# Two hybrid transformer blocks in one kernel: the pool of the weights begins 64 bytes further in SBUF

## Chip, cores and metric

One Trainium2 chip, one core. The metric is the device time of one execution in microseconds (us). The kernel before takes 2362.53 us, the median of 3 runs (2360.72 to 2367.87). The compute engines are called by their names in the profile: PE (TensorE; PEld is its weight load, the LDWEIGHTS instruction that goes ahead of each matmul), DVE (VectorE), ACT (ScalarE), POOL (GpSimd); SP is the engine from whose queue the weights' transfers are issued.

## What is computed

256 tokens of width 1024 go through two layers of a first block and two of a second, all in float32. Cut to what matters here (the attention branches in between are left out):

```python
for l in range(2):                                   # first block
    h = rms(x, ln1[l]) * (1 + sc1) + sh1
    x = x + g1 * mixing(h @ w_in[l], ...) @ w_o[l]
    h = rms(x, ln2[l]) * (1 + sc2) + sh2
    x = x + g2 * ((silu(h @ w_gate[l]) * (h @ w_up[l])) @ w_down[l])
for l in range(2):                                   # second block, 256 tokens and 256 of a context
    h, hc = norm(x) * (1 + scale) + shift, norm(ctx) * (1 + scale_c) + shift_c
    parts, parts_c = split(h @ w_in[l]), split(hc @ w_in[l])
    y = g_a * (y_a @ w_a_out[l]) + g_b * (y_b @ w_b_out[l]) + g_c * (y_c @ w_c_out[l])
    x = x + gate * (y @ w_out[l])
```

Nearly all of the work is in the dense products with `w_in`, `w_o`, `w_gate`, `w_up`, `w_down`, and the second block's `w_in`, `w_*_out`, `w_out`.

## The kernel before

**Dense products.** Every factor of a dense product is held as two tiles of type fp32r, a rounded part (`hi`) and the rest (`lo`), and a product is the sum of three matmuls per 128 rows of the contraction: hi·hi, hi·lo, lo·hi (`mm3`, L559). All matmuls go through one recording helper, so that the profile shows L170 for each; they are told apart by their tiles. In a name such as `ps_mm<-h,whi`, the first tile behind the arrow is the one that streams through the array (the moving operand), the second the one that was loaded as weights (the stationary operand).

- `dense_t` (L570): 128 columns of the weights are stationary, the inputs move, 256 or 512 columns wide (`ps<-h,whi`). It is used for the first block's `w_o`, `w_gate`, `w_up`, `w_down`, for part of its `w_in`, and for most of the second block.
- `dense_n` (L576): 128 tokens of the inputs are stationary, 256 columns of the weights move (`ps<-whi,h`). It is used for those projections that are wanted token by token.

**Tiles and where they lie.** A block of weights is fetched by SP into one of two `raw` tiles (`fetch`, L356), and then split in two halves (`split_half`, L381): ACT rounds `raw` into `whi`, DVE (sometimes POOL) writes `raw - whi` into `wlo`. There are two of each, 8192 bytes per partition, all six in the pool `w` (L1854). The normed inputs of all dense products lie in `h2`, two tiles of 16384 bytes (L1866), in a pool that is stacked from the other end of SBUF, as are the tiles of the feed-forward part (`ahi`, `alo`, L1175), the gated branches (`part`) and the merged output (`fhi`, `yacc`). The pools opened behind `w` on its own side (conditioning, masks, `dft`, `u`, `pq`, the attention tiles of the left side) follow it in the stack.

All block sizes and steps of these tiles are multiples of 512 bytes, so that the byte at which a matmul's operand starts, modulo 512, is the same for every block of a tile. In the program these bytes are:

| tile | start modulo 512 | distance from the weights, around 512 |
|---|---|---|
| `whi`, `wlo`, `raw` | 160 | |
| `h` (a slice of `h2`), `part`, `fhi`, `yacc` | 480 | 192 |
| `ahi`, `alo`, first block's layer 0 | 288 | 128 |
| `ahi`, `alo`, first block's layer 1 | 384 | 224 |
| `dft`, `u`, `pq` (they meet each other only) | 64 | (0 from each other) |

**The order of the work.** While the program is built, a planner (`Clock`, L66, and `Pipe`, L222) keeps a modelled time for each engine and decides from it in which order instructions are written to the queues. It knows tiles by name and by offsets inside a tile; where a tile lies in SBUF does not enter.

The function that the diff touches, and its callers:

Of the kernel before, what the change touches and what calls it, by code (L numbers as in the profile page):

```python
# [7 lines left out]
F32 = mybir.dt.float32  # L8
# [295 lines left out]
class Program:  # L304
# [1544 lines left out]
    def run(self):  # L1849
# [2 lines left out]
        self.const = self.stack.enter_context(self.pool("const"))  # L1852
        self.x = self.const.tile([128, KC, L], F32, name="xT")
        self.wp = self.stack.enter_context(self.pool("w"))  # L1854
        self.gbufs = 4
        self.gw = None
        self.dram = self.stack.enter_context(tc.tile_pool(name="dram", bufs=1, space=bass.MemoryType.DRAM))
# [216 lines left out]
```

## Time and profile before

| | |
|---|---|
| median of 3 runs | 2362.53 us |
| the profiled execution, own time | 2364.57 us |
| its span, first to last instruction | 2362.8 us |
| mean granted TensorE clock | 0.969 of full speed |
| PE, PEld busy | 2247.8 us (95%), 1974.9 us (84%) |
| DVE, ACT, POOL busy | 1287.4 (54%), 1032.1 (44%), 371.7 us (16%) |

A matmul's duration in the profile (mean ns) runs from its start to the modelled end of its results, and the next one begins while it still runs. So the quantity to read is the pace: the time from the start of one matmul to the start of the next, in an unbroken stretch a window's length by its number of matmuls. A window counts every matmul that overlaps it, so that two or three at its ends are counted too many (280 ns of duration against a pace below 120 ns).

### The profile page before, as it was taken

The numbers are of one execution on the slowest core, as the hardware profiler recorded it, in microseconds if no ns is written. First come the engines' busy times: TensorE is split into PE (matmuls) and PEld (weight loads), VectorE is DVE, ScalarE is ACT, GpSimd is POOL, SyncE is SP. The second block draws the span as 40 slices with busy tenths as digits, with TensorE's granted clock in tenths as the row PEclk, the third lists the DMA queues.
The fourth block names the chain that finished last, engine by engine and source line by source line (L and its number), as shares of the span: only waits on it lengthen the run. The fifth ranks groups of instructions, "written<-read, shape, count | busy, mean of one in ns | idle before, by whom it ended". The sixth has DMA issues, their size and how long they took to land. (4 is left out here: it accounts for less than half of the span.)

```text
span 2362.8 us, 39015 instructions
## 1 busy us (share of the span) xinstructions
PE 2247.8 (95%) x15672; PEld 1974.9 (84%) x15672; DVE 1287.4 (54%) x2547; ACT 1032.1 (44%) x1994; POOL 371.7 (16%) x897
## 2 busy tenths in 40 slices
PE   7989999998899999997989999999999999989999
PEld 3756899876899988887878888888898897989999
DVE  3735556575556546666554424335364656655665
ACT  3543445445444444554543323223254445444543
POOL 3311001551000103122022000000020333220000
PEclk8978999998999999998999999999999999999999
DMA  9646985655686522122114434434343232337865
GB/s 331 230 159 220 288 252 181 212 188 196 197 243 187 173 89 72 56 82 72 61 65 139 128 91 113 119 94 114 96 131 90 81 99 74 106 114 201 211 172 170
DMA packets 395061, 348.52 MB, mean 148 GB/s; under 512 B 12768, under 2 KB 364384, under 8 KB 394368
## 3 DMA queue, kind: packets, MB, share of 16 engines
q1 hardware_dynamic: 386752, 321.29, 45.1%
q0 software_dynamic: 6688, 21.66, 2.9%
q10 hardware_dynamic: 1440, 3.08, 0.4%
q8 instruction: 123, 2.02, 0.4%
q14 instruction: 58, 0.48, 0.1%
HBM read 335.50 MB, written 10.49 MB: 146 GB/s over the span
## 5 line engine op out<-in xcount | busy, mean ns | idle before, releaser
L170 DVE TENSOR_TENSOR wlo<-raw,whi 128x1024 fp32r<-128x1024 f32 (+1 forms) x465 | 547.6, 1210 | 449.1 <-ACT whi L170 447.8
L170 ACT CAST whi<-raw 128x1024 fp32r<-128x1024 f32 (+3 forms) x476 | 471.5, 1031 | 216.1 <-PE ps_t L170 63.3
L170 PE MATMUL ps_mm<-whi,h 128*128 128x256 f32 x2752 | 533.9, 291 | 16.1 <-ACT whi L170 6.2
L170 PEld LDWEIGHTS ps_mm<-whi,h 128*128 128x128 f32 x2752 | 440.6, 194 | 48.7 <-issue 19.3
L170 PE MATMUL ps_mm<-wlo,h 128*128 128x256 f32 x1376 | 391.1, 284 | 7.5 <-DVE wlo L170 7.3
L170 PE MATMUL ps_mm<-h,whi 128*128 128x256 f32 (+2 forms) x1656 | 375.5, 321 | 1.9 <-DVE xT L170 1.8
L170 PEld LDWEIGHTS ps_mm<-h,whi 128*128 128x128 f32 (+1 forms) x1656 | 269.2, 187 | 46.9 <-issue 9.0
L170 PEld LDWEIGHTS ps_mm<-wlo,h 128*128 128x128 f32 x1376 | 266.8, 194 | 12.6 <-DVE wlo L170 8.4
L170 PE MATMUL ps_mm<-h,wlo 128*128 128x256 f32 (+2 forms) x828 | 263.0, 318 | 1.1 <-POOL wlo L170 1.1
L170 PE MATMUL ps_s<-h,whi 128*128 128x256 f32 (+1 forms) x1120 | 240.2, 310 | 0.0
L170 PE MATMUL ps_t<-h,whi 128*128 128x256 f32 (+1 forms) x1096 | 234.9, 310 | 2.1 <-ACT h L170 1.5
L170 PEld LDWEIGHTS ps_s<-h,whi 128*128 128x128 f32 x1120 | 181.3, 188 | 18.3 <-ACT th L170 5.6
L170 PEld LDWEIGHTS ps_t<-h,whi 128*128 128x128 f32 x1096 | 179.0, 190 | 19.8 <-ACT th L170 6.3
L170 PE MATMUL ps_s<-h,wlo 128*128 128x256 f32 (+1 forms) x560 | 173.4, 310 | 0.1
L170 PE MATMUL ps_t<-h,wlo 128*128 128x256 f32 (+1 forms) x548 | 169.5, 309 | 0.0
L170 PEld LDWEIGHTS ps_mm<-h,wlo 128*128 128x128 f32 (+1 forms) x828 | 155.1, 187 | 14.7 <-POOL wlo L170 1.3
L170 PE MATMUL ps_g<-gw,c 128*32 128x512 f32 (+1 forms) x640 | 100.8, 640 | 18.0 <-DMA gw<-in_w_mod_dram 8.7
L170 PEld LDWEIGHTS ps_s<-h,wlo 128*128 128x128 f32 x560 | 105.2, 188 | 7.0 <-DVE wlo L170 0.3
L170 PEld LDWEIGHTS ps_t<-h,wlo 128*128 128x128 f32 x548 | 104.2, 190 | 6.2 <-DVE wlo L170 0.2
L170 ACT ACTIVATE M<-ps_s,nmB,rsB 128x512 f32<-128x512 f32 (+1 forms) x96 | 67.0, 702 | 94.2 <-DVE nmB L170 94.2
L170 DVE SCALAR_TENSOR_TENSOR y<-th,y 128x512 f32<-128x512 f32 (+1 forms) x64 | 35.6, 556 | 81.2 <-ACT th L170 67.9
L170 POOL TENSOR_TENSOR sqa<-sqa,sq 128x256 f32<-128x256 f32 x30 | 22.1, 736 | 346.9 <-ACT sq L170 191.3
(406 smaller groups left out, 3726.8 us busy)
## 6 DMA issues: line engine op xcount, KB each, us to landing
raw<-in_w_in_dram SPq DMA_DIRECT2D x72, 1024.0 KB, 5.3
raw<-in_w_in_dram SPq DMA_DIRECT2D x100, 512.0 KB, 4.1
gw<-in_w_mod_dram SPq DMA_DIRECT2D x96, 512.0 KB, 5.3
gw<-in_w_ada_dram SPq DMA_DIRECT2D x64, 384.0 KB, 5.0
raw<-in_w_gate_dram SPq DMA_DIRECT2D x44, 512.0 KB, 4.1
raw<-in_w_up_dram SPq DMA_DIRECT2D x44, 512.0 KB, 5.6
raw<-in_w_down_dram SPq DMA_DIRECT2D x16, 1024.0 KB, 5.1
raw<-in_w_out_dram SPq DMA_DIRECT2D x12, 1024.0 KB, 5.2
```

Of the source, the lines that this page charges most:

```text
L170: return real(*a, **k)
```

## The change

One tile of 16 float32 per partition, 64 bytes, is allocated as the first of the pool `w`. Nothing reads or writes it. The six tiles of the weights, and everything that is stacked behind them on their side, lie 64 bytes further; the tiles on the other side stay. Weights then start at 224 modulo 512, and `h`, `part`, `fhi` and `yacc`, still at 480, are 256 bytes from them.

```diff
         self.x = self.const.tile([128, KC, L], F32, name="xT")
         self.wp = self.stack.enter_context(self.pool("w"))
+        self.wp.tile([128, 16], F32, name="apart")
         self.gbufs = 4
```

## Rows read from the trace of the kernel before

**Rows 1.** The page, parts 1 and 2: busy time, and PE in 40 slices.
```profile
PE 2247.8 (95%) x15672; PEld 1974.9 (84%) x15672; DVE 1287.4 (54%) x2547; ACT 1032.1 (44%) x1994; POOL 371.7 (16%) x897
...
PE   7989999998899999997989999999999999989999
...
PEclk8978999998999999998999999999999999999999
```

**Rows 2.** Groups of instructions by shape, PE: matmuls with weights; busy us, mean ns.
```profile
L170 PE MATMUL ps_mm<-whi,h 128*128 128x256 f32 x2752 | 533.9, 291 | 16.1 <-ACT whi L170 6.2 <-ACT h L170 5.5 <-DVE pq L170 2.1
L170 PE MATMUL ps_mm<-wlo,h 128*128 128x256 f32 x1376 | 391.1, 284 | 7.5 <-DVE wlo L170 7.3 <-POOL wlo L170 0.2
L170 PE MATMUL ps_mm<-h,whi 128*128 128x256 f32 x1112 | 203.9, 284 | 1.9 <-DVE xT L170 1.8
L170 PE MATMUL ps_mm<-h,whi 128*128 128x512 f32 x512 | 161.6, 397 | 0.0
...
L170 PE MATMUL ps_s<-h,wlo 128*128 128x256 f32 x408 | 113.8, 279 | 0.1
...
L170 PE MATMUL ps_s<-alo,whi 128*128 128x256 f32 x132 | 37.1, 281 | 0.0
...
L170 PE MATMUL ps_t<-alo,whi 128*128 128x256 f32 x110 | 30.9, 281 | 0.0
...
L170 PE MATMUL ps_mm<-part,whi 128*128 128x256 f32 x144 | 25.6, 278 | 0.0
...
L170 PE MATMUL ps_mm<-part,wlo 128*128 128x512 f32 x56 | 22.0, 392 | 0.0
...
L170 PE MATMUL ps_s<-part,wlo 128*128 128x256 f32 x56 | 15.6, 279 | 0.0
```

**Rows 3.** The chain of waits, pieces in order of time: start us, us, what.
```profile
2203.03 2.83 PE ps_mm L170 x24
...
2318.55 2.72 PE ps_t L170 x24
```

**Rows 4.** Unbroken stretches of PE: window, its length, PE busy (count), granted clock, DMA.
```profile
703.00:745.00 42.00, 42.00 (x373) 1.00 0.68 193
2181.00:2228.00 47.00, 47.00 (x402) 1.00 0.77 199
1251.00:1258.00 7.00, 7.00 (x64) 1.00 0.13 43
1932.00:1940.00 8.00, 8.00 (x70) 1.00 0.17 44
746.00:807.00 61.00, 61.00 (x518) 1.00 0.62 194
370.00:396.00 26.00, 26.00 (x221) 1.00 0.59 190
1410.00:1498.00 88.00, 88.00 (x386) 1.00 0.44 117
```

**Rows 5.** Timeline of PE in the second block's Fourier branch: start us, us, what.
```profile
1265.35 1.60 PE L170 MATMUL ps_mm<-dft,u 128*128 128x256 f32 x12
```

**Rows 6.** The same windows view: first and last runs of each pace.
```profile
43.70:46.30 2.60, 2.60 (x25) 1.00 1.05 354
2080.40:2082.70 2.30, 2.30 (x23) 1.00 0.00 0
71.80:74.20 2.40, 2.40 (x22) 1.00 0.67 259
2097.00:2102.00 5.00, 5.00 (x45) 1.00 0.26 90
195.50:197.80 2.30, 2.30 (x23) 1.00 0.60 168
2338.00:2359.00 21.00, 21.00 (x188) 1.00 0.40 128
54.60:59.80 5.20, 5.20 (x47) 1.00 1.03 367
2271.00:2296.00 25.00, 25.00 (x214) 1.00 0.57 163
```


## The prediction

> **What bounds the kernel now.** I read the page's busy times first, then its slices, then the groups by shape, and then went from durations to paces. PE is busy for 95% of the span, and in the slices nearly always for nine tenths or more, while DVE stands at 54% and ACT at 44% [rows 1]. The chain of waits at the end of the kernel is almost nothing but matmuls, in pieces of 24 without a gap [rows 3]. So PE bounds it, and what counts is the pace at which one matmul follows another in an unbroken stretch.
>
> Two kinds carry most of it: 256 columns wide with the weights moving (`h` stationary), 2752 + 1376 = 4128 matmuls, and with the weights stationary. Of the latter `h` moves in six groups, from 1112 matmuls to 408, together 4128, and `part`, `fhi` or `yacc` in fifteen, from 144 to 56, together 1152, which makes 5280. `ahi` and `alo` make nine groups, from 132 to 110, together 1056. 512 columns wide are twelve groups, from 512 to 56, together 2208 [rows 2].
>
> [...] With weights stationary a piece of 24 takes 2.83 us in one stretch and 2.72 us in another, 117.9 and 113.3 ns each [rows 3]; long windows give the same, 47 us by 402 less the 2.4 at its ends is 117.6 ns, 42 us by 373 less 2.4 is 113.3 ns. With weights moving the same two paces return: 7 us by 61.6 (113.6 ns) and 8 us by 67.6 (118.3 ns) [rows 4]. I call them 113.3 and 117.8. DMA, at a share of 0.13 to 0.77 in these windows, doesn't sort them [rows 4].
>
> Other operands have other paces in the same shape. With `ahi` and `alo` moving it is 61 us by 515.6, 118.3 ns, in layer 1 and 26 us by 218.6, 118.9 ns, in layer 0 [rows 4]. With `dft` and `u` twelve matmuls span 1.60 us, of which the last one's duration is 0.28 us [rows 2], so that eleven intervals take 120.0 ns each [rows 5]. None of the three shows 113.3. The shape is the same; what differs is where the tiles lie. 512 columns come at 88 us by 384.3, 229.0 ns [rows 4].
>
> How often is each pace held? I sorted all unbroken runs of at least twelve equal matmuls. Weights moving: 79 runs with 2187 matmuls near 113.3 (first 43.7, last 2080.4 us), 52 runs with 1461 near 117.8 (first 71.8, last 2097 us), a mean of 115.1 ns. Weights stationary: 19 runs with 1006 near 113.3 (first 195.5, last 2338 us), 82 with 3967 near 117.8 (first 54.6; 2271 us is among the last), a mean of 116.9 ns [rows 6].
>
> **The change part by part.** *The new tile* is neither written nor read: no instruction, no wait, no transfer. The planner doesn't see addresses, so every queue, SP's and POOL's with it, keeps its order. Cost nothing, and it needs no cover.
>
> *The transfers, casts and subtractions on the weights* work on `raw`, `whi` and `wlo`, which move together by 64 bytes. I see no reason for another duration. If some became longer, the 46% and 56% in which DVE and ACT are idle [rows 1] would cover it; with that cover gone, it would show as PE waiting for `wlo` or `whi`, now 7.3 and 6.2 us in the largest groups [rows 2]. I take 0.
>
> *Distances.* `h`, `part`, `fhi`, `yacc` go from 192 to 256 bytes from the weights, `ahi` and `alo` from 128 to 64 (layer 0) and from 224 to 160 (layer 1), `dft` and `u` stay at 0, since they move together. No row shows a distance of 256. The bounds for the pace at 256 columns are the rows at hand: below, 113.3 for all; above, the 120.0 at distance 0.
>
> Which is nearest? Order the five pairs by distance modulo 512: 0 gives 120.0; 128 gives 118.9; 192 gives 113.3 or 117.8; 224 gives 118.3. That isn't monotone, since 224 is worse than 192. Taken modulo 128 it is: 0 and 128 are both 0 and are the slow ones, 224 is 32 from a multiple and lies between, 192 is 64 from one and is the only one that reaches 113.3. A repeat of 128 bytes is thus the simplest reading of rows 3 to 5, and by it 256 falls in with 0 and 128, in the worst class. I take the middle of 118.6 (2.847 us for 24, a little under layer 0's 118.9, whose window holds a start) and 120.0, 119.3 ns, for all of these pairs.
>
> The sum: weights stationary 5280 x (119.3 - 116.9) = 12.7 us; weights moving 4128 x (119.3 - 115.1) = 17.3 us; layer 0's half of `ahi` and `alo`, 528 matmuls, comes to 64 and gains 528 x (118.9 - 116.9) = 1 us; layer 1's stays 32 from a multiple, 0. [...] Its bounds are 2 x 113.3 and 113.3 + 120.0, that is -5 to +9.5 us for 2208. Together 29 us. Where a run ends in a wait for another engine, a slower pace eats idle time first; PE is idle for 5% of the span and more often in the short runs with weights moving, so I count nine tenths, 26 us.
>
> The profiled execution has a span of 2362.8 us and a time of 2364.57 us, 2.0 us above the median of 2362.53. I put the sum on the median: 2362.5 + 26 = 2388.5, say 2388 us. The case's own range: 118.6 everywhere gives 9 + 14.4 - 1 = 22.4, by 0.85 19 us; 120.0 everywhere with 9.5 for the wide ones gives 16.4 + 20.2 + 9.5 = 46, by 0.95 44 us; if the place of the moving operand alone decides, and only the weights' own place is now bad, the moving half gives 17.3 x 0.85 = 15 us. So 2376 to 2406.
>
> [...] Rows 4 and 5 show one shape at paces from 113.3 to 120.0 ns, split by tiles. [...]
>
> **The rivals.**
>
> *Faster: distance counts modulo 512, and the farther the better.* Place: the same matmuls. For it: 0, 128 and 192 do improve in this order (120.0, 118.9, then 113.3 to 117.8), and 256 is as far as tiles can lie. Against it: 224 is farther than 192 and holds 118.3 over 515 matmuls, without a stretch of 113.3. It decides from the point at which the runs now at 117.8 fall to 113.3. Price: 5280 x (116.9 - 113.3) = 19.0 and 4128 x (115.1 - 113.3) = 7.4 us, with 0 to 5 us from the wide ones 26 to 31 us, by nine tenths 24 to 28: 2337 us.
>
> *No change: distance is not the cause.* Two paces occur at one and the same distance [rows 4], so something else, such as the moment at which a run starts, chooses between them, and may go on doing so with the same shares. Or the place of the moving operand itself is what matters: `h` stays at 480, and the weights at 224 agree with it modulo 256. Or the empty tile is dropped and nothing moves. Against it: three pairs at other distances never reach 113.3. Price: 0, with a few us for runs that lock otherwise: 2362 us, 2356 to 2369.
>
> **How the numbers follow.** Slower 0.43, no change 0.26, faster 0.31. A measurement of this kernel can tell about 0.3% from no change, 7 us here, and the prices of both moving cases are well beyond it. The predicted time is that of the likeliest case, 2388 us, whose own range is 2376 to 2406. The range for all: up to 2404, which leaves out 0.04, and down to 2337, the centre of the faster case, which leaves out half of it, 0.16.
>
> **What would show it.** In the profile after, the count of instructions must be the same. In the stretch that is now 2181 to 2228 us pieces of 24 with `h` moving should take 2.85 to 2.88 us instead of 2.83, and none 2.72; with the weights moving no run should hold 113.3 ns. `dft` and `u` must stay at 120.0 ns, since their distance does: if they change too, it is their own place that counts and not the distance. Layer 0's `ahi` and `alo` should reach 113.3 or 117.8. The forecast is wrong if pieces of 24 with `h` are at 2.72 us throughout (faster), if both paces stay with their shares (no change), or if the pace does as I say and the time doesn't follow, in which case PE isn't the bound that I take it for.

## The result, and the profile after

The changed kernel takes 2381.66 us, the median of 4 runs (2378.66 to 2388.73), against 2361.62 for the kernel before beside it (4 runs, 2353.09 to 2367.87): a ratio of 1.0092 with a 95% interval of 1.0067 to 1.0116, slower by 20 us. The profiled execution took 2378.66 us, with a span of 2376.9 us.

The page, parts 1 and 2 (busy us, share of the span, instructions; PE and its granted clock in 40 slices), to be read against [rows 1]:

```profile
PE 2261.7 (95%) x15672; PEld 1999.1 (84%) x15672; DVE 1289.3 (54%) x2547; ACT 1031.1 (43%) x1994; POOL 370.4 (16%) x897
...
PE   7979999998999999997989999999999998999999
...
PEclk8989999999999999998999999999999999999999
```

The counts are the same on every engine. DVE, ACT and POOL are within 2 us of before; PE has 13.9 us more and its weight load 24.2 us more. Casts and subtractions did not become longer, and no other engine took over.

The groups of PE by shape (busy us, mean ns of one, idle before), against [rows 2]:

```profile
L170 PE MATMUL ps_mm<-whi,h 128*128 128x256 f32 x2752 | 547.6, 294 | 16.2 <-ACT whi L170 5.8 <-ACT h L170 5.8 <-DVE h L170 2.2
L170 PE MATMUL ps_mm<-wlo,h 128*128 128x256 f32 x1376 | 395.4, 287 | 6.3 <-DVE wlo L170 6.3
L170 PE MATMUL ps_mm<-h,whi 128*128 128x256 f32 x1112 | 208.3, 287 | 2.1 <-DVE xT L170 1.6
L170 PE MATMUL ps_mm<-h,whi 128*128 128x512 f32 x512 | 160.9, 395 | 0.0
...
L170 PE MATMUL ps_s<-alo,whi 128*128 128x256 f32 x132 | 36.9, 280 | 0.0
```

With 256 columns both kinds are longer by about 3 ns of duration, the 512-wide ones shorter by 2 and `alo` by 1. The waits ahead of them are within about 1 us of what they were.

The chain of waits (start us, us, what), in the stretch of [rows 3] and near the end:

```profile
2203.51 2.88 PE ps_mm L170 x24
...
2364.79 2.88 PE ps_t L170 x24
```

24 matmuls take 2.88 us, 120.0 ns each, where there had been 2.83 and 2.72. There is no other length left: each full piece of this chain from 2197 to 2370 us is 2.88 or 2.89.

Windows of unbroken stretches (window, its length, PE busy and count, granted clock, DMA share, GB/s). The first five are to be read as [rows 4], the last one is a stretch early in the kernel:

```profile
2190.00:2237.00 47.00, 47.00 (x394) 1.00 0.76 193
700.00:742.00 42.00, 42.00 (x352) 1.00 0.64 178
746.00:804.00 58.00, 58.00 (x497) 1.00 0.61 192
362.00:387.00 25.00, 25.00 (x214) 1.00 0.59 191
1423.00:1491.00 68.00, 68.00 (x302) 1.00 0.46 120
100.00:200.00 100.00, 85.81 (x588) 0.91 0.62 210
```

47 us by 394 less the 2.4 at the ends is 120.0 ns, and 42 us by 349.6 is 120.1: the two stretches that had held 117.6 and 113.3 are now equal. `ahi` and `alo` are at 58 by 494.6, 117.3 ns, in layer 1, and at 25 by 211.6, 118.1 ns, in layer 0 (that window holds a start; inside it they come at 117.8). 512 columns are faster: 68 us by 300.3 is 226.4 ns, where it was 229.0.

The timeline of PE (start us, us, what), two starts of the lo·hi product with the weights moving, 23 such rows apart, and the Fourier branch as in [rows 5]:

```profile
1254.04 0.28 PE L170 MATMUL ps_mm<-wlo,h 128*128 128x256 f32 x1
...
1262.32 0.28 PE L170 MATMUL ps_mm<-wlo,h 128*128 128x256 f32 x1
...
1269.18 1.60 PE L170 MATMUL ps_mm<-dft,u 128*128 128x256 f32 x12
```

8.28 us for 23 x 3 matmuls is 120.0 ns for the weights moving too. `dft` and `u`, whose distance did not change, still take 1.60 us for 12.

**Where the 20 us are.** Both kernels issue the same 15,672 matmuls in the same order, so each interval from one start to the next can be set against its counterpart. Taking intervals that are regular in both (below 150 ns, 260 for the wide ones): weights stationary +15.4 us, weights moving +15.9, `ahi` and `alo` -1.0, 512 columns -4.4, together +25.9 us. All other matmuls and the breaks give -11.9, and the whole from first to last start is +14.0, as the spans say. Of those -11.9, 10.8 us lie in the small matmuls at the beginning, before 235 us, where the profiled execution of before had a low granted clock. Its row there, to be read against the last one above:

```profile
100.00:200.00 100.00, 86.58 (x514) 0.80 0.54 182
```

514 matmuls at a clock of 0.80 against 588 at 0.91. That part goes by the execution rather than by the pace of the dense products: the executions profiled for the experiments below have 0.80 to 0.90 in this window, and the mean clock of the kernel before alone goes from 0.967 to 0.979 over its runs. With one profile for each kernel it isn't shown that the places have no part in it. From the matmul that starts at 235.1 us before and at 224.7 us after to the last one, the two take 2124.0 and 2148.4 us: 24.4 us more, close to the 25.9 us of the paces. The medians, 20 us apart, are between the 14 us of the two whole profiles and the 25.9 us.

### The profile page after: what moved, and what is told of

It is laid out like the page before. It is cut to its first block, busy times and chain, and to the rows that moved or that the text cites. A ratio compares the mean times of both kernels' runs of the same rounds, so it can differ in the third digit from the quotient of the medians.

```text
span 2376.9 us, 39015 instructions
## 1 busy us (share of the span) xinstructions
PE 2261.7 (95%) x15672; PEld 1999.1 (84%) x15672; DVE 1289.3 (54%) x2547; ACT 1031.1 (43%) x1994; POOL 370.4 (16%) x897
## 3 DMA queue, kind: packets, MB, share of 16 engines
q1 hardware_dynamic: 386752, 321.29, 45.2%
## 5 line engine op out<-in xcount | busy, mean ns | idle before, releaser
L170 PE MATMUL ps_mm<-whi,h 128*128 128x256 f32 x2752 | 547.6, 294 | 16.2 <-ACT whi L170 5.8
L170 PEld LDWEIGHTS ps_mm<-whi,h 128*128 128x128 f32 x2752 | 446.9, 195 | 48.6 <-issue 19.3
L170 PE MATMUL ps_s<-h,whi 128*128 128x256 f32 (+1 forms) x1120 | 245.3, 315 | 0.0
L170 PE MATMUL ps_g<-gw,c 128*32 128x512 f32 (+1 forms) x640 | 95.0, 607 | 16.7 <-DMA gw<-in_w_mod_dram 7.8
```

The costliest lines, as they stand in the source:

```text
L170: return real(*a, **k)
```

## Experiments

What was open: whether the distance is the cause at all, or a place of its own of one tile; with which period it counts; and whether the sign counts. In what follows the difference is the start of the stationary operand less that of the moving one, modulo 256. For the weights (`w`) and inputs (`h`) the same two tiles thus have two differences, one for each kind of product. Paces without a fence are means over the starts of unbroken sequences of ten equal matmuls in the trace. Each ratio is against the kernel before as it ran beside the changed one, with medians of 2357 to 2364 us.

**The inputs moved instead of the weights.** The weights stay at 160, `h` goes to 416, and they are again 256 apart.

```diff
+        p2.tile([128, 16], F32, name="apart2")
```

> The weights stay at 160 modulo 512; the inputs and everything on their side lie 64 bytes lower instead (h at 416), so that the distance is 256 as in the kernel after. Theory A (the distance between the two operands modulo 128 sets the pace): pieces of 24 at 2.88 us as after, no run at 113.3 ns, ratio to before 1.007 to 1.012. Rival B (the weights' own place is what is bad at 224): both paces 113.3 and 117.8 as before, ratio 0.997 to 1.003.

Measured: 2381.79 us, ratio 1.0084 (1.0064 to 1.0104). From the chain of waits:

```profile
2203.54 2.88 PE ps_t L170 x24
```

All paces are those of the changed kernel: 120.0, 226.7 for 512 columns, 117.8 and 117.3 for `ahi` and `alo`. So the empty tile in the pool of the weights is not the point, nor the place of the weights; that of the inputs could as well be moved.

**Both moved.** Weights at 224, `h` at 416: they are 192 apart as before, but in the places that each of them had in a slower kernel.

```diff
+        self.wp.tile([128, 16], F32, name="apart")
...
+        p2.tile([128, 16], F32, name="apart2")
```

> Weights at 224 as in the kernel after, inputs at 416: the distance is 192 again. Theory A: paces 113.3 and 117.8 with shares like before, ratio 0.997 to 1.003; ahi and alo of layer 0, now at the same place as the weights, at 118.6 to 120 ns. Rival B (the weights' own place): 120.0 ns throughout, ratio 1.007 to 1.012.

Measured: 2365.73 us, ratio 1.0008 (0.9989 to 1.0026): the 20 us are gone. But the paces are not those of before. From the chain, and two windows (with `h` moving 512 wide, with `ahi` and `alo`):

```profile
2203.24 2.72 PE ps_s L170 x24
```

```profile
1414.00:1485.00 71.00, 71.00 (x306) 1.00 0.44 116
733.00:795.00 62.00, 62.00 (x519) 1.00 0.60 190
```

Here the stretch near 2200 us, 2.83 in [rows 3], runs at 2.72. Weights stationary now mostly hold 113.3 (mean 114.1 ns) and weights moving mostly 117.8: the two kinds have exchanged their paces. 512 columns are at 71 by 304.3, 233.3 ns, and `ahi` and `alo` of layer 1 at 62 by 516.6, 120.0. The sign explains it. Before, weights stationary had 160 - 480, which is 192 modulo 256, and weights moving the reverse, 64; here it is 224 - 416 = 64 (modulo 256) for the one and 192 for the other. `ahi` and `alo` have come to a difference of 0 in layer 0 (224 - 224) and of 160 in layer 1 (224 - 320, modulo 256), and to 120.0 in both. The gains and losses cancel (-13.8 + 8.0 + 1.5 + 9.4 us).

**The same distances at other places.** Two more kernels with `w` - `h` = 64 (modulo 256), at 192 and 384, and at 256 and 448.

```diff
+        self.wp.tile([128, 8], F32, name="apart")
...
+        p2.tile([128, 24], F32, name="apart2")
```

> Distance 192 as before, but the inputs start at a multiple of 128 (384) and the weights 64 beyond one (192), by 32 bytes more on the weights' side and 96 on the inputs'. Theory A (distance modulo 128 alone): paces 113.3 and 117.8 in some mixture, ratio 0.990 to 1.003. Theory E (where the moving operand starts within 128 bytes chooses between these two: at 0 or 32 it holds 113.3, at 64 or 96 it holds 117.8): weights stationary, moving operand at 0, 113.3 ns throughout; weights moving, at 64, 117.8 ns; 5280 x -3.6 + 4128 x 2.7 = -8 us, ratio 0.994 to 0.999.

Measured: 2363.82 us, ratio 1.0011 (0.9993 to 1.0030).

```diff
+        self.wp.tile([128, 24], F32, name="apart")
...
+        p2.tile([128, 8], F32, name="apart2")
```

> The other way round, inputs at 448 (64 beyond a multiple of 128), weights at 256 (a multiple). Theory A: a mixture, ratio 0.990 to 1.003, the same as for the run before it. Theory E: weights stationary at 117.8, weights moving at 113.3 ns; 5280 x 0.9 - 4128 x 1.8 = -3 us, ratio 0.997 to 1.001.

Measured: 2368.02 us, ratio 1.0022 (0.9999 to 1.0045). From the chains of the first and the second of the two:

```profile
2202.16 2.72 PE ps_mm L170 x24
```

```profile
2202.62 2.72 PE ps_s L170 x24
```

Every pace is that of the kernel with both moved: 113.3 for most weights stationary, 117.8 for most weights moving, 233.3 for 512 columns. Three pairs of places, one difference, one set of paces. A theory by which the moving operand's own start within 128 bytes decides, expected the second kernel to part from the first, with 117.8 where 113.3 came; it falls.

**The weights 256 bytes further**, to 416, in place of 64.

```diff
+        self.wp.tile([128, 64], F32, name="apart")
```

> The pool of the weights begins 256 bytes further than before: weights at 416, 64 bytes from the inputs. Theory A (repeat of 128 bytes): 64 is as good as 192, paces 113.3 and 117.8, ratio 0.997 to 1.003; layer 0's ahi and alo at distance 128 stay at 118.6 to 120. Rival C (repeat of 512 bytes, only 192 away is good, near is bad): 119 to 120 ns, ratio 1.006 to 1.012.

Measured: 2360.75 us, ratio 0.9993 (0.9979 to 1.0008).

```profile
2204.27 2.83 PE ps_mm L170 x24
```

All paces are those of before, though the tiles' distance modulo 512 is now 64 and not 192. The period is 256 bytes or a divisor of it.

**The weights 32 bytes further**, to 192.

```diff
+        self.wp.tile([128, 8], F32, name="apart")
```

> The pool begins 32 bytes further: moving less stationary operand is 32 modulo 128 with weights stationary and 96 with weights moving. Theory A: weights stationary at 117.3 ns (as layer 1's ahi and alo after the change, also 32), weights moving at 118.3 ns (as the same before the change, 96), neither 113.3 nor 120.0 in long runs; 5280 x 0.4 + 4128 x 3.2 = 15 us by nine tenths, ratio 1.004 to 1.008. Rival D (only whole 64 byte steps count): paces as before, ratio 0.997 to 1.003.

Measured: 2378.05 us, ratio 1.0070 (1.0046 to 1.0095). Windows of weights stationary, of `ahi` and `alo` of layer 1, and of 512 columns:

```profile
2193.00:2239.00 46.00, 46.00 (x396) 1.00 0.77 200
740.00:799.00 59.00, 59.00 (x523) 1.00 0.64 200
1420.00:1491.00 71.00, 71.00 (x306) 1.00 0.44 116
```

46 by 393.6 is 116.9 ns (difference 224), a little less than the 117.8 of before; weights moving (32) are at 118.3; `ahi` and `alo` of layer 1, now at 64, at 59 by 520.6, 113.3 ns, those of layer 0, at 160, at 120.0. The paces 256 wide came within 1 ns of what was expected, and 118.3 and 116.7 to 116.9 are not the paces of before, so that the rival falls. 512 columns at 233.3 did not come as expected: they were to stay, and their 9 us are half of the sum of the paces. Without them it would be 8 us, or 0.3%, below the expected range: that the time lay in it is luck.

**Distance 128 for both kinds**: weights at 256, `h` at 384. A period of 128 wants 120.0 and 226.7 here, as at 0.

```diff
+        self.wp.tile([128, 24], F32, name="apart")
...
+        p2.tile([128, 24], F32, name="apart2")
```

> Inputs at 384 and weights at 256, both multiples of 128, distance 128. Theory A: 120.0 ns as after, 512 columns at 226.7 ns as after, ratio 1.007 to 1.012. Rival H (what counts is that no tile starts 32 bytes off a multiple of 64): 113.3 ns, ratio 0.988 to 0.995.

Measured: 2380.29 us, ratio 1.0072 (1.0047 to 1.0098). From the chain, and the window of 512 columns:

```profile
2204.11 2.85 PE ps_t L170 x24
```

```profile
1429.00:1499.00 70.00, 70.00 (x302) 1.00 0.42 117
```

The time alone would pass for the period of 128, the paces don't: 2.85 and not 2.88 (118.7 ns for either kind), and 70 by 300.3, 233.1 ns, where 226.7 was wanted. Nor is it the 113.3 of the rival. 128 is a class of its own: in these runs the period is 256 in full.

**The lo half alone moved.** Only `wlo` starts 64 bytes further, so that in each product two of three matmuls keep their difference.

```diff
-                t = self.wp.tile([128, KC * WB], F32R, name=f"{nm}{j % 2}")
-                self.blk[j][i] = t[:, :kch * n].rearrange("p (k c) -> p k c", k=kch)
+                t = self.wp.tile([128, KC * WB + 128], F32R, name=f"{nm}{j % 2}")
+                o = 16 if i == 2 else 0
+                self.blk[j][i] = t[:, o:o + kch * n].rearrange("p (k c) -> p k c", k=kch)
```

> Only the two wlo tiles lie 64 bytes further (at 224), whi stays at 160: of three matmuls with weights stationary one loads wlo while h moves beside whi. Theory A with the pair being the load under way and the moving operand: the matmul that runs while wlo is loaded, the one before the lo matmul, costs 120, the others 113.3 to 117.8; mean of 24 at 2.77 to 2.85 us, ratio 0.999 to 1.005. Rival F (the pair is a matmul's own two operands): the lo matmul itself is the longer one. Rival G (any one pair in the row sets the pace of all): 120.0 throughout, ratio 1.007 to 1.012.

Measured: 2371.02 us, ratio 1.0031 (1.0017 to 1.0045). With weights stationary the interval that begins with the matmul on `wlo` takes 119.9 ns (`h` moving, 1284 intervals), that from `whi` to `wlo` 117.0 and that from `whi` to `whi` 116.5. So with weights stationary it is the matmul's own two operands that count, one matmul at a time, and not those of its neighbour; a theory by which one bad matmul in three holds all three at 120 falls. With the weights moving the runs don't show this: 119.3 from `wlo` on, 118.8 into it, 117.1 between the others, where all three had been 115.3 to 115.5. There the matmuls on `whi` became slower too, though their own difference had stayed at 64, and why stays open.

**Steps of 16 bytes.** All weights 112 and 144 bytes further, inside tiles made wider by 512 bytes (differences of 48 and 208, and of 80 and 176), to see whether the pace goes smoothly from one neighbour to the next. Theory I in what was expected is that the pace is a function of the difference modulo 256, with one value for each difference; its list stands in what was expected of the last experiment.

```diff
-                self.blk[j][i] = t[:, :kch * n].rearrange("p (k c) -> p k c", k=kch)
+                self.blk[j][i] = t[:, 28:28 + kch * n].rearrange("p (k c) -> p k c", k=kch)
```

> All weights 112 bytes further inside their tiles: stationary less moving is 48 with weights stationary and 208 with weights moving, modulo 256. By theory I, between its neighbours (32 118.3 and 64 113.3; 192 117.8 and 224 116.7): 114 to 118 and 116 to 118 ns, ratio 0.998 to 1.006. Rival J (what is between multiples of 32 bytes is worse, since an operand then begins inside 32 bytes): above 118.3 in both, ratio over 1.006.

Measured: 2388.06 us, ratio 1.0131 (1.0103 to 1.0158).

```diff
-                self.blk[j][i] = t[:, :kch * n].rearrange("p (k c) -> p k c", k=kch)
+                self.blk[j][i] = t[:, 36:36 + kch * n].rearrange("p (k c) -> p k c", k=kch)
```

> All weights 144 bytes further inside their tiles: stationary less moving is 80 with weights stationary and 176 with weights moving, modulo 256. By theory I, between its neighbours (64 113.3 and 96 117.3; 160 120.0 and 192 117.8): 113.3 to 117.3 and 117.8 to 120 ns, ratio 0.997 to 1.007. Rival J: above 118.3 in both, ratio over 1.006.

Measured: 2389.93 us, ratio 1.0138 (1.0119 to 1.0157). From the chains of the first and the second:

```profile
2203.79 2.84 PE ps_s L170 x24
```

```profile
2202.62 2.85 PE ps_s L170 x24
```

It doesn't go smoothly. A difference of 48 lies between 118.3 (at 32) and 113.3 (at 64) and has two paces: 117.7 to 118.3 in 29 long runs with 3717 intervals, as in the first row above, and 123.0 in 26 with 1284, the longest pace of this case (at a granted clock of 1.00; a mean of 119.3). 80 lies between 113.3 and 117.3 (at 96) and measures 118.7; 208 lies between 117.8 and 116.7 and measures 118.4. The others of this series (16, 144, 176, 240) are between their neighbours or level with one, so that the rival's ratio came but its rule doesn't hold for them. At 176 the two kinds of product part: 119.2 with the weights moving, 118.1 with `ahi` and `alo` of layer 1. These are the slowest kernels of all: 16 bytes to either side of 64, nothing is left of its gain.

**Each block where its use wants it.** If the signed difference modulo 256 is the cause, a block of weights can be put at 64 from what it meets, or at 0 where it is used 512 wide, without moving any tile.

```diff
+def place(pieces):
+    name, l, r, c, w = pieces[0]
+    if name in ("w_o", "w_gate", "w_out_2"):
+        return 128
+    if name == "w_down":
+        return 32 if l else 192
+    if name == "w_in":
+        return 128 if c in (QB, QB + 256) else 0
+    if name == "w_in_2":
+        if c < AV:
+            return 64
+        if AO <= c < BQ or BZ <= c < CU or c >= CZ:
+            return 128 if l else 64
+    return 0
...
+            o = place(pieces) // 4
-                t = self.wp.tile([128, KC * WB], F32R, name=f"{nm}{j % 2}")
-                self.blk[j][i] = t[:, :kch * n].rearrange("p (k c) -> p k c", k=kch)
+                t = self.wp.tile([128, KC * WB + 128], F32R, name=f"{nm}{j % 2}")
+                self.blk[j][i] = t[:, o:o + kch * n].rearrange("p (k c) -> p k c", k=kch)
```

> The weights' tiles stay at 160, but each block is written at a place in them that depends on its use, so that stationary less moving is 64 modulo 256 for all products 256 columns wide (as for weights moving before the change) and 0 for those 512 wide. Theory I (the pace is a function of stationary less moving modulo 256: 0 120.0, 32 118.3, 64 113.3 with some 117.8, 96 117.3, 128 118.7, 160 120.0, 192 117.8 with some 113.3, 224 116.7 ns): weights stationary 5280 x (114.2 - 116.9), ahi and alo 1056 x (113.5 - 118.5), 512 columns 2208 x (226.7 - 228.9), together -24 us, by nine tenths -22: ratio 0.988 to 0.993, below both kernels. Theory A (modulo 128): the distance of h is as good as before, gain from ahi, alo and the wide ones alone, ratio 0.994 to 0.999.

Measured: 2341.35 us (12 runs, 2334.81 to 2354.78), ratio 0.9935 (0.9916 to 0.9953). It beats both kernels. From the chain, and windows of `ahi` and `alo` of layer 1 and of 512 columns:

```profile
2203.26 2.72 PE ps_t L170 x24
```

```profile
735.00:793.00 58.00, 58.00 (x514) 1.00 0.64 202
1404.00:1473.00 69.00, 69.00 (x306) 1.00 0.46 120
```

Weights stationary are at 2.72 throughout this stretch, `ahi` and `alo` of layer 1 at 58 by 511.6, 113.4 ns, and 512 columns at 69 by 304.3, 226.7. The paces came as meant, with two exceptions: `ahi` and `alo` of layer 0, also at 64, stayed at 117.8, and a few blocks placed for 512 columns are used 256 wide too, at 119.8. The time fell by 0.65%, less than was expected, and its interval reaches into the range of theory A; what decides between the two is the pace, since by theory A `h` would have stayed at 117.8 and 2.83.

**All runs side by side.** The regular intervals, each against its counterpart of before, in us, and in percent of before's 2362.8 us; beside them the measured ratio as a percentage:

| kernel | weights stationary | moving | `ahi`, `alo` | 512 wide | sum | sum, % | measured, % |
|---|---|---|---|---|---|---|---|
| the change | 15.4 | 15.9 | -1.0 | -4.4 | 25.9 | 1.10 | 0.92 |
| inputs moved | 15.4 | 16.0 | -1.0 | -4.3 | 26.1 | 1.10 | 0.84 |
| both moved | -13.8 | 8.0 | 1.5 | 9.4 | 5.1 | 0.22 | 0.08 |
| the same, 192 and 384 | -13.3 | 7.2 | 1.5 | 9.3 | 4.7 | 0.20 | 0.11 |
| the same, 256 and 448 | -13.5 | 7.6 | 1.5 | 9.4 | 5.0 | 0.21 | 0.22 |
| 256 further | 2.0 | -1.1 | 0.0 | 0.2 | 1.1 | 0.05 | -0.07 |
| 32 further | -0.6 | 10.7 | -2.0 | 9.3 | 17.4 | 0.74 | 0.70 |
| distance 128 | 8.9 | 12.3 | -2.4 | 9.0 | 27.8 | 1.18 | 0.72 |
| lo half alone | 4.5 | 11.2 | -0.6 | 0.3 | 15.4 | 0.65 | 0.31 |
| 112 further | 12.4 | 11.0 | 0.9 | 9.2 | 33.5 | 1.42 | 1.31 |
| 144 further | 9.3 | 13.8 | -0.3 | 6.5 | 29.3 | 1.24 | 1.38 |
| by use | -15.4 | -1.0 | -3.1 | -4.4 | -23.9 | -1.01 | -0.65 |

The sum of the paces gives the sign wherever the interval of the measured ratio leaves out 1; the measured change is then from a half of the sum to a little more than all of it. No run took the remaining difference apart; the profiles show waits ahead of weights moving that shrink as the pace grows (for the change -3.5 us in the breaks of that kind).

## Why the prediction was right, and where it was not

*What bounds the kernel.* It held: with the same counts and the same work on the other engines, a slower pace of PE came out as time.

*The new tile itself, the transfers, casts and subtractions:* taken as 0, and they were: the largest DMA queue at 45.2% of its 16 engines' span after 45.1%, DVE 1.9 us more, ACT 1.0 less, waits for `wlo` and `whi` within 1 us of [rows 2].

*The pace at the new distance* was put at 119.3 ns between bounds of 118.6 and 120.0; it is 120.0 with the weights stationary and 119.8 with them moving. The upper bound, taken from `dft` and `u` [rows 5], was the right row, since those two are at a difference of 0 as well. By the formula of the prediction this makes 5280 x 3.1 = 16.4 and 4128 x 4.7 = 19.4 us in place of 12.7 and 17.3; the intervals themselves give 15.4 and 15.9, since not all are in regular runs.

*512 columns, taken as 0 between bounds of -5 and +9.5 us*, is the term that was mis-sized: -4.4 us, near the lower bound, at 226.7 ns, twice 113.3. No run shows the 0 as a rule: over the runs 512 columns take from 226.7 to 233.3 ns by the difference, -4.4 to +9.4 us. *Layer 0's half of `ahi` and `alo`* came to 117.8 as one of the two paces named, and gained 0.5 us; *layer 1's*, taken as 0, gained as much. Together +25.9 in place of +29.

*Nine tenths of it:* 26 us were forecast, 20 us is the ratio of the medians; the two profiles alone show 14. What separates the 14 from the 25.9 of the paces is mostly the beginning of the profiled executions (-10.8), and the shorter waits ahead of weights moving (-3.5), which are the idle time that the prediction meant. Without the beginning it is 24.4. The interval of the ratio reaches from 16 to 27 us, so that neither 24.4 nor nine tenths of 25.9, 23 us, can be told from the 20 of the medians, and the factor itself stays untested.

*The repeat of 128 bytes* is the step that failed as a rule. That it gave the right class for this change is luck: 256 falls in with 0 by a period of 256 as well, but not with 128. With a difference of 128 the pace is 118.7, not 120.0, and 512 columns take 233.3, not 226.7. In these runs the period is 256 (with the weights 256 bytes further 24 take 2.83 us again) and the difference has a sign: at 64 most 256-wide runs hold 113.3 and fewer 117.8, at 192 it is the other way round. That, too, is why the two kinds of product had different shares of the two paces [rows 6], which the prediction left to the way in which a run starts. It sorted its rows by a distance without a sign, and so read 192 for both.

*The rivals.* Modulo 512, the farther the better: 2337 us would have needed 113.3 where 120.0 came, and 256 bytes more changed nothing. No change because distance is not the cause: two tiles moved apart by either side give one time, moved together give it back. The moving operand's own place: `h` at 416, 384 and 448 has given the same paces at a difference of 64, and at 480 and 416 at a difference of 0.

For operands of type fp32r the runs show one shape, weights stationary, mostly at 113.3 ns where the two operands' starts differ by 64 modulo 256 (three pairs of places), and at 120.0 where they differ by 0 (two pairs). Why the pace goes with this difference, and why modulo 256, no run here shows. It also stays open what chooses between 113.3 and 117.8, or 118.0 and 123.0, where both occur.

## What to carry to other kernels

Where a kernel is bound by matmuls that each load new weights, read the pace from the starts in an unbroken stretch and compare it between pairs of tiles of one shape; if it differs, look at the operands' start addresses, stationary less moving, modulo 256. This is shown for one core, operands of type fp32r and 128 rows; for others no run here shows it. An offset inside a wider tile is a cheap way to choose it for each block, and worth 0.65% here; but choose by the width of the matmul, and measure, since of the differences between multiples of 32 bytes none was better than its better neighbour, and a pad of 64 bytes cost 0.9% here without an instruction changing.

## What the runs showed that was not expected

The pace by the difference of the operands' starts, stationary less moving, modulo 256 (granted clock 1.00, fp32r, 128 rows; in brackets the pace that fewer of the runs hold):

| difference, bytes | 256 columns, ns | 512 columns, ns |
|---|---|---|
| 0 | 120.0 | 226.7 |
| 32 | 118.3 | |
| 64 | 113.3 (117.8) | 233.3 |
| 96 | 117.3 | |
| 128 | 118.7 | 233.3 |
| 160 | 120.0 | |
| 192 | 117.8 (113.3) | 228.9 |
| 224 | 116.7 | 233.3 |
| 16, 48, 80 | 118.3, 118.0 (123.0), 118.7 | for 48 and 80: 233.3, 232.0 |
| 144, 176, 208, 240 | 120.0, 119.2, 118.4, 118.8 | |

The table is not a law without exceptions: at 64 `ahi` and `alo` of layer 0 held 117.8 in the last experiment and a mean of 115.8 in the one at distance 128, and at 176 those of layer 1 held 118.1.

A difference of 0, with 160 the worst for 256 columns among the multiples of 32, is the best for 512; 64, the best for 256, is among the worst for 512. Either of these two serves one width and costs the other, which is why the kernel with both tiles moved gained 14 us in one kind and lost 19 in the others.
